# Column fetches, depth blocks and small sums put at other places in a one-core mLSTM and attention trunk

## The chip, the cores and the metric

The kernel runs on one core of a Trainium2 chip. The metric is the device time of one execution in microseconds (us). TensorE is called PE below, VectorE DVE, ScalarE ACT, SyncE SP.

## What is computed

Two layers act on x, 512 tokens of 2048 columns, in float32. Each layer normalises x over its columns, scales and shifts it by columns that are made from a conditioning vector c, runs a mixer, normalises the mixer's output and adds it to x, times a gate column. The first mixer is an mLSTM with 8 heads, the second an attention over bands of chunks with 16 heads, whose keys and values come from the stream after the first layer.

```
sc = silu(c)
for l in (0, 1):
    shift, scale, gate = split(sc @ ada_w[l] + ada_b[l])
    h = rmsnorm(x, g_pre[l]) * (1 + scale) + shift
    if l == 0:
        y = mlstm(h @ a_w_in) @ a_w_out                # 8 heads
    else:
        kshift, kscale = split(sc @ kv_ada_w + kv_ada_b)
        kv = (rmsnorm(x, kv_g) * (1 + kscale) + kshift) @ kv_w
        y = (band_attention(h @ b_w_in, kv) * silu(z)) @ b_w_out   # 16 heads
    x = x + gate * rmsnorm(y, g_post[l])
```

## The kernel before

**Precision and weights.** All projections are made from pairs of tiles: a number is split into a high part (an ACT cast, line 182) and a low part (a DVE subtraction, line 183), and a product is three matmuls: high by high, high by low, low by high (`mm3`, line 226). Weights lie in DRAM in the order of their use (`stream`, line 60). Each call of `wpiece` (line 188) takes the next piece: an SP transfer into a raw buffer (line 200; two buffers, and in some stages a third), then the split. All transfers are issued by SP, one after the other.

**Order.** The instructions are given to a scheduler that orders each engine's list by the program and by priorities (`tc.high_priority`). An instruction that is pinned (`pin`, `tc.keep_in_program_order`) stays behind what the program has put on its engine so far. What is not pinned may go ahead.

**Modulation columns.** The 128 groups of 128 columns (shift, scale and gate of the layers, shift and scale of the keys) are not made by PE. For each group a transfer brings rows of the transposed weights (`ada_load`, line 376, halves of 512 KB), and DVE multiplies them with a broadcast of silu(c) and sums (`ada_sum`, line 381, one instruction for a half). They are spread over the program as background work.

**Start** (lines 401 to 453). c is fetched, then the four quarters of x (line 409), 1 MB each, then constants and the first four halves of columns, for depth tile 0. PE broadcasts c and ACT makes silu(c) from it (line 420). ACT squares x, DVE adds the squares (lines 433 and 436), PE sums them over the partitions (`token_sums`, line 424), and the reciprocal root is spread over a tile by four small products and matmuls (`dg`, lines 448 to 450).

**First projection** (lines 460 to 477). Depth tiles k = 0 to 15 come in BLOCKS: 0-1, 2-5, 6-9, 10-13, 14-15. For each k, four column halves are loaded and summed and the input h is made (`modulated`, line 357: a DVE pass, an ACT pass, a DVE pass at line 360); then PE does the lead, 6 column tiles of weights (18 matmuls of 512 columns) that accumulate in six PSUM banks through all blocks. After the lead of a block, ten later column tiles follow with all k of the block; each is added by DVE to an accumulator in SBUF (line 477).

**Heads, then the first output projection.** Heads 0 to 7 run with columns as background. From each head's output, the square sum over its columns is split and summed by PE (`sums`, line 546; called at line 745). The output projection (`rows`, line 861) goes by groups g of 512 columns; a weight piece covers two depth tiles (24 matmuls with four row tiles). `proj_b` (line 245) calls a function at given depth steps k0 (its `at`). In g = 0 and in the first pair of row tiles of g = 1 to 3, `scale_sums` (line 872) is such a function: it sums the four quarters of scale columns that its last call loaded, and loads the next four. The inputs y of the projection are fetched piece by piece (line 777).

**Keys and values.** Values first, then eight key tiles with `proj_s` (line 266), which computes pairs of depth tiles with seven half products instead of eight (`seven`) where the sums of inputs are ready, and plainly (`eight`) elsewhere. KEY_PAIRS says for how many of eight pairs. `input_sums` (line 929) makes the sums of one more pair.

**Tail.** After attention comes `b_w_out`, again by groups g of 512 columns; group 3 goes in two halves, rows 0-1 and rows 2-3. `gate_steps` (line 1178) places the gate columns' loads and sums (`gate_sums`), their transposes (`gate_part`, which runs `gates_out`, line 572: a DVE product, a PE transpose, a store), the reading back as a row (`gate_row`), and the product with group 0's output (`gate_first`, line 1173). `fetch_x` (line 1126) fetches the stored stream; `finish` (line 1146) ends a row tile.

Of the kernel before, what the change touches and what calls it, by code (L numbers as in the profile page):

```python
# [15 lines left out]
P = 128  # L16
D = 2048
S = 512
# [17 lines left out]
PAIRS = [(0, 1), (2, 3)]  # L36
BLOCKS = [(0, 2), (2, 6), (6, 10), (10, 14), (14, 16)]
LEAD = [0, P, V0 // 2, V0 // 2 + P, O0, O0 + P]
# [3 lines left out]

KEY_PAIRS = [6, 7, 8, 8, 8, 8, 8, 8]
HEAD_PAIRS = 6
# [88 lines left out]
def hybrid_trunk(ctx, tc, xT, xN, c, adaT, cols, wst, wg, ext, kc, out):  # L133
# [42 lines left out]
    def col(i):  # L176
        return cl[:, i : i + 1]
# [176 lines left out]
    def newa(name):  # L354
        return psA.tile([P, S], F32, tag="a", name=name)
# [59 lines left out]
    early = [ada_load(KT, j, ap_, ADA_BUFS, pin) for j in range(2)]  # L415
    early += [ada_load(0, j, sp, 4, pin) for j in range(2)]
    for i in range(4):
        ps = newp(f"ps_c{i}")
        mm(ps, ones_f[0:1, :], crow[i], True, True)
        nc.scalar.activation(scB[:, i * S : (i + 1) * S], ps, AF.Silu)  # L420
    nc.sync.dma_start(csc, scB[0:1, :])
    pss = newa("ps_x")

# [4 lines left out]
    for q in range(4):  # L428
        pair = []
        for i in range(2):  # L430
            sq = xp.tile([P, 2, S], F32, tag="x", name=f"xsq{q}_{i}")
            nc.scalar.activation(sq, xq[q][:, 2 * i : 2 * i + 2, :], AF.Square)
            pin(nc.vector.tensor_tensor(sq[:, 0, :], sq[:, 0, :], sq[:, 1, :], op=ALU.add))
            pair.append(sq[:, 0, :])
        if q < 3:
            pin(nc.vector.tensor_tensor(pair[0], pair[0], pair[1], op=ALU.add))
            token_sums(pair[0], q == 0, False)
        else:
            token_sums(pair[0], False, False)
            token_sums(pair[1], False, True)  # L440
    rc = sp.tile([P, 4], F32, name="rc")
    nc.scalar.activation(rc, pss[:, 0:4], AF.Sqrt, bias=eps_c, scale=1.0 / D)
    for a in early[:2]:
        ada_sum(*a, pin)
    pin(nc.vector.reciprocal(rc, rc))
    psr = newa("ps_rb")
    for m in range(4):
        dg = tp.tile([P, S], F32, tag="t", name=f"dg{m}")[:, :P]
        pin(nc.vector.tensor_scalar(dg, ident, rc[:, m : m + 1], None, op0=ALU.mult))
        mm(psr[:, m * P : (m + 1) * P], ones_f, dg, m == 0, m == 3)  # L450
    nc.scalar.copy(rstd0, psr)
    for a in early[2:]:
        ada_sum(*a, pin)
    h1 = []
# [90 lines left out]

    def sums(ps, x, name, early=0):
# [4 lines left out]
        mm(ps, ones_r, t[:, 0, :], True, False)  # L551
        mm(ps, ones_r, t[:, 1, :], False, True)

# [77 lines left out]
    for h in range(NH):  # L631
# [239 lines left out]

    def scale_sums():

        for i, j, a in scale_in:
            pin(nc.vector.tensor_tensor_reduce(
                a, a, scQ[j], 1.0, mod[:, i : i + 1] if j else col(CB + i), ALU.mult, ALU.add, mod[:, i : i + 1]
            ))
        scale_in.clear()
        for i, j in scale_cols[:4]:
            d = slice(j * S, (j + 1) * S)  # L880
            if len(scQ) == j:
                scQ.append(tp.tile([P, S], F32, tag="t", name=f"scQ{j}"))
                pin(nc.sync.dma_start(scQ[j], csc[0, d].partition_broadcast(P)))
            a = tp.tile([P, S], F32, tag="t", name=f"adq{i}_{j}")
            pin(nc.sync.dma_start(a, adaT[i, :, d]))
            scale_in.append((i, j, a))
        del scale_cols[:4]
# [285 lines left out]
    def gate_first():  # L1173
# [83 lines left out]
```

## Time and profile before

| | |
|---|---|
| median of 3 runs (lowest, highest) | 2802.58 us (2798.52, 2809.12) |
| profiled execution, its own time | 2803.29 us |
| its span | 2801.5 us |
| PE, DVE, ACT busy | 99%, 77%, 49% of the span |
| moved by DMA | 527.09 MB, mean 188 GB/s |

A span is the time from the first to the last record of one execution. A busy share is an average over stages with different limits; a stage is read by windows of time. In a list of waits each row names the engine and line that stood still, what released it, the time in total, the number of times and the longest. In a timeline a row gives the start, the busy time, the engine, the line, the operation with output and inputs, how many were merged, and in brackets the idle time before it with what ended it. Matmuls overlap, so their merged busy times are longer than their pace.

### The profile page before, as it was taken

What the parts mean: (1) busy time and instruction counts of PE and PEld (TensorE: products, weight loads), DVE (VectorE), ACT (ScalarE), POOL (GpSimd) and SP (SyncE); (2) the same over time, 40 slices, a digit from 0 to 9 for tenths busy, and PEclk for the clock granted to TensorE, in tenths of its full rate; (3) what the DMA queues carried; (4) which work ended last, traced back from release to release, by engine and by line L of the source; (5) the groups of instructions that cost most, each with busy time, mean ns of one, the idle gap of its engine ahead of it and who ended that gap; (6) DMA issues with size and microseconds to landing.
All of it is one profiled execution on the core that took longest, in us unless ns stands there. A gap on an engine that the chain in (4) does not pass through costs nothing.

```text
span 2801.5 us, 42223 instructions
## 1 busy us (share of the span) xinstructions
PE 2765.5 (99%) x15959; PEld 2439.5 (87%) x15959; DVE 2156.6 (77%) x3788; ACT 1370.5 (49%) x2032; POOL 0.2 (0%) x4
## 2 busy tenths in 40 slices
PE   7999999999999999999999999999999999999998
PEld 5887888888998989989998788888998899999886
DVE  6986978769786876858867577567986788898666
ACT  4234524234454554545545344568534566666523
POOL 0000000000000000000000000000000000000000
PEclk9999999999999999999999999999999999999999
DMA  7875697865232332323324889778535534434876
GB/s 289 308 259 180 213 319 249 300 224 181 91 114 93 102 115 91 113 91 106 120 85 140 280 292 306 260 257 297 175 131 175 174 125 129 130 122 126 291 266 207
DMA packets 182999, 527.09 MB, mean 188 GB/s; under 512 B 19669, under 2 KB 38133, under 8 KB 182153
## 3 DMA queue, kind: packets, MB, share of 16 engines
q1 hardware_dynamic: 182794, 524.38, 55.4%
q8 instruction: 125, 2.05, 0.3%
q14 instruction: 80, 0.66, 0.1%
HBM read 490.69 MB, written 38.85 MB: 189 GB/s over the span
## 4 chain that ended last, share of the span: by engine, by line
PE 85%; DVE 6%; DMA 5%; issue 2%; ACT 2%; SPq 0%; DVEq 0%; ACTq 0%
PE ps_y L224 14%; PE ps_v L224 12%; PE ps_kv L224 5%; PE ps_azo L224 5%; PE ps_o L224 4%; PE ps_bzo L224 3%; PE ps_az L224 3%; PE ps_cz L224 3%; PE ps_dz L224 3%; PE ps_qk L224 3%; PE ps_z L224 3%; PE ps_czo L224 3%; PE ps_dzo L224 3%; PE ps_s L224 2%; DMA wr<-in_wst 2%
## 5 line engine op out<-in xcount | busy, mean ns | idle before, releaser
L182 ACT CAST wh<-wr 128x1024 fp32r<-128x1024 f32 (+3 forms) x586 | 585.4, 1001 | 709.5 <-PE ps_y L224 152.5
L183 DVE TENSOR_TENSOR wl<-wr,wh 128x1024 fp32r<-128x1024 f32 (+3 forms) x586 | 679.0, 1161 | 307.3 <-ACT wh L182 300.4
L224 PE MATMUL ps_y<-wh,y 128*128 128x512 f32 x1536 | 477.3, 390 | 1.3 <-ACT y L182 1.1
L182 ACT CAST wsh<-ws 128x384 fp32r<-128x384 f32 (+1 forms) x261 | 163.4, 626 | 372.7 <-issue 137.1
L224 PEld LDWEIGHTS ps_y<-wh,y 128*128 128x128 f32 x1536 | 288.2, 188 | 62.3 <-ACT y L182 1.5
L224 PE MATMUL ps_v<-wh,h 128*128 128x512 f32 x1024 | 322.1, 390 | 0.4 <-DVE zq L318 0.4
L224 PE MATMUL ps_y<-wl,y 128*128 128x512 f32 x768 | 299.2, 390 | 0.7 <-DVE wl L183 0.7
L183 DVE TENSOR_TENSOR wsl<-ws,wsh 128x384 fp32r<-128x384 f32 (+1 forms) x261 | 181.8, 696 | 125.8 <-ACT wsh L182 124.1
L224 PEld LDWEIGHTS ps_v<-wh,h 128*128 128x128 f32 x1024 | 192.3, 188 | 40.2 <-DVE zq L318 0.8
L224 PE MATMUL ps_v<-wl,h 128*128 128x512 f32 x512 | 199.6, 390 | 0.0
L224 PEld LDWEIGHTS ps_y<-wl,y 128*128 128x128 f32 x768 | 144.2, 188 | 30.6 <-DVE wl L183 1.2
L224 PE MATMUL ps_kv<-wh,hkv 128*128 128x512 f32 x512 | 159.4, 390 | 0.0
L207 DVE TENSOR_TENSOR ws<-wr 128x256 f32<-128x256 f32 (+1 forms) x261 | 132.1, 515 | 30.8 <-DMA wr<-in_wst 28.7
L382 DVE CUSTOM_DVE_ANT_0 ada<-ada,scB,mod 128x1024 f32<-128x1024 f32 x96 | 123.0, 1282 | 17.5 <-DMA ada<-in_adaT 16.6
L382 DVE CUSTOM_DVE_ANT_0 ada<-ada,scB,cl 128x1024 f32<-128x1024 f32 x96 | 122.9, 1281 | 14.7 <-DMA ada<-in_adaT 14.7
L224 PEld LDWEIGHTS ps_kv<-wh,hkv 128*128 128x128 f32 x512 | 96.1, 188 | 19.8
L224 PEld LDWEIGHTS ps_v<-wl,h 128*128 128x128 f32 x512 | 96.2, 188 | 19.7 <-issue 0.9
L224 PE MATMUL ps_azo<-h,wh 128*128 128x256 f32 (+1 forms) x406 | 101.4, 331 | 0.4 <-DVE zo L318 0.4
L224 PE MATMUL ps_l<-h,wh 128*128 128x512 f32 x320 | 99.2, 392 | 1.0 <-ACT oz L475 1.0
L224 PE MATMUL ps_kv<-wl,hkv 128*128 128x512 f32 x256 | 99.7, 390 | 0.0
L224 PE MATMUL ps_czo<-h1s,wsh 128*128 128x256 f32 x468 | 89.3, 283 | 0.0
L209 DVE TENSOR_TENSOR ws<-wr 128x128 f32<-128x128 f32 (+1 forms) x261 | 85.2, 336 | 3.6
(389 smaller groups left out, 6259.9 us busy)
## 6 DMA issues: line engine op xcount, KB each, us to landing
wr<-in_wst SPq DMA_DIRECT2D x520, 512.0 KB, 3.7
ada<-in_adaT SPq DMA_DIRECT2D x224, 512.0 KB, 5.9
adq<-in_adaT SPq DMA_DIRECT2D x64, 256.0 KB, 5.4
xt<-nsc SPq DMA_DIRECT2D x48, 256.0 KB, 3.7
yr<-ysc SPq DMA_DIRECT2D x16, 512.0 KB, 3.8
wr<-in_wst SPq DMA_DIRECT2D x30, 256.0 KB, 4.6
wr<-in_wst SPq DMA_DIRECT2D x16, 384.0 KB, 7.8
bsc<-in_ext SPq DMA_DIRECT2D x16, 320.0 KB, 6.4
```

The source lines that it names most:

```text
L182: nc.scalar.copy(hi, src)
L183: nc.vector.tensor_tensor(lo, src, hi.bitcast(F32), op=ALU.subtract)
L207: nc.vector.tensor_tensor(t[:, : 2 * w], r[:, w : 3 * w], r[:, : 2 * w], op=ALU.subtract)
L209: nc.vector.tensor_tensor(t[:, 2 * w :], r[:, 3 * w :], r[:, w : 2 * w], op=ALU.subtract)
L224: nc.tensor.matmul(ps, a, b, start=start, stop=stop)
L382: pin(nc.vector.tensor_tensor_reduce(at, at, (sc or scB)[:, j * D // 2 : (j + 1) * D // 2], 1.0, mod[:, i : i + 1] if j else col(CB + i), ...
```

## The change

- The constants `cols` and the first four column halves are fetched before x, and summed before anything of x. The last quarter of x comes in two halves; of its squares ACT makes two and DVE two. The four `dg` products write one tile.
- BLOCKS are 0-1, 2-4, 5-8, 9-12, 13-15.
- `scale_sums` loads two quarters a step at twice as many steps, and sums a batch two steps after its load; the last ones are summed at the beginning of the second pair of row tiles.
- The two matmuls of the last head's square sum get a lower priority.
- The first key tile no longer makes another input sum: KEY_PAIRS is 6, 6, 7, 8 and so on in place of 6, 7, 8, 8.
- Gate loads begin four depth steps earlier in group 0, and the later steps are put earlier; `gate_first` goes from the last half of group 3 to the half before it; the fetches of the stored stream are pinned and put at other steps.

```diff
-BLOCKS = [(0, 2), (2, 6), (6, 10), (10, 14), (14, 16)]
+BLOCKS = [(0, 2), (2, 5), (5, 9), (9, 13), (13, 16)]
...
-KEY_PAIRS = [6, 7, 8, 8, 8, 8, 8, 8]
+KEY_PAIRS = [6, 6, 7, 8, 8, 8, 8, 8]
...
+    pin(nc.sync.dma_start(cl, cols))
+    early = [ada_load(i, j, *where, pin) for j in range(2) for i, where in ((KT, (ap_, ADA_BUFS)), (0, (sp, 4)))]
...
-        pin(nc.sync.dma_start(t, xT[q]))
+        for d in [slice(0, 4)] if q < 3 else [slice(0, 2), slice(2, 4)]:
+            pin(nc.sync.dma_start(t[:, d, :], xT[q, :, d, :]))
...
-        if q == 1:
-            pin(nc.sync.dma_start(cl, cols))
     pin(nc.sync.dma_start(kcs, kc[:, :144]))
-    early = [ada_load(KT, j, ap_, ADA_BUFS, pin) for j in range(2)]
-    early += [ada_load(0, j, sp, 4, pin) for j in range(2)]
...
     nc.sync.dma_start(csc, scB[0:1, :])
+    for a in early:
+        ada_sum(*a, pin)
...
+            for i in range(2):
+                nc.scalar.activation(sq[i][:, 0, :], xq[q][:, 2 * i, :], AF.Square)
+                pin(nc.vector.tensor_tensor(sq[i][:, 1, :], xq[q][:, 2 * i + 1, :], xq[q][:, 2 * i + 1, :], op=ALU.mult))
...
-    for a in early[:2]:
-        ada_sum(*a, pin)
     pin(nc.vector.reciprocal(rc, rc))
     psr = newa("ps_rb")
+    dg = xp.tile([P, 4, P], F32, tag="x", name="dg")
...
-    for a in early[2:]:
-        ada_sum(*a, pin)
...
+        with tc.high_priority(-late):
+            mm(ps, ones_r, t[:, 0, :], True, False)
+            mm(ps, ones_r, t[:, 1, :], False, True)
...
-        sums(ps, sqs, f"q{h}", AHEAD if h == NH - 1 else 0)
+        sums(ps, sqs, f"q{h}", *((AHEAD, 80) if h == NH - 1 else ()))
...
+    def scale_sums(n=1):
+
+        while len(scale_in) > n:
+            for i, j, a in scale_in.pop(0):
...
-        for i, j in scale_cols[:4]:
+        batch = []
+        for i, j in scale_cols[:2]:
...
-    rows(0, range(4), y_tile, {k: scale_sums for k in (6, 12, 18, 24, 30)})
+    rows(0, range(4), y_tile, {k: scale_sums for k in (*range(4, 32, 4), 30)})
...
-            at = {k: scale_sums for k in ((6, 14, 22, 30) if g < 3 else (6, 14, 22))} if pair == 0 else {}
+            at = {k: scale_sums for k in range(2, 32, 4)} if pair == 0 else {}
             if pair == 0 and g == 3:
-                at[30] = lambda: (scale_sums(), amul_cols(2, 48 + KT, GPRE + KT))
+                at |= {28: scale_sums}
+            if pair == 1 and g == 1:
+                scale_sums(0)
+                amul_cols(2, 48 + KT, GPRE + KT)
...
-        at = {2: input_sums} if ready < KT // 2 else {}
+        at = {2: input_sums} if i and ready < KT // 2 else {}
...
-            nc.sync.dma_start(t[i], xsc[m, :, 2 * i * S : 2 * (i + 1) * S].rearrange("p (a t) -> p a t", a=2))
+            pin(nc.sync.dma_start(t[i], xsc[m, :, 2 * i * S : 2 * (i + 1) * S].rearrange("p (a t) -> p a t", a=2)))
...
-        0: {14: gate_begin},
-        1: {2: gate_sums, 6: gate_sums, 8: lambda: gate_part(1), 12: lambda: (gate_row(1, 1), gate_sums())},
-        2: {2: gate_sums, 4: lambda: gate_part(2), 6: gate_sums, 8: lambda: gate_row(1, 2), 12: gate_sums, 14: lambda: gate_part(3)},
-        3: {0: gate_sums, 4: lambda: gate_row(1, 3), 8: gate_sums, 10: lambda: gate_part(0), 14: lambda: gate_row(1, 0, late[1])},
+        0: {10: gate_begin},
+        1: {0: gate_sums, 4: gate_sums, 6: lambda: gate_part(1), 10: lambda: (gate_row(1, 1), gate_sums()), 12: lambda: fetch_x(0), 14: gate_sums},
+        2: {0: lambda: gate_part(2), 2: gate_sums, 4: lambda: (gate_row(1, 2), fetch_x(1)), 6: gate_sums, 8: lambda: gate_part(3), 10: gate_sums, 12: lambda: fetch_x(2), 14: gate_sums},
+        3: {0: lambda: gate_part(0), 2: lambda: (gate_row(1, 3), fetch_x(3)), 6: lambda: gate_row(1, 0, late[1]), 12: gate_first},
...
-            at = {2: gate_first, 4: lambda: finish(0), 6: lambda: finish(1)} if pair == PAIRS[1] else {}
-            if 0 < g < 3:
-                at = {k: lambda k=k: fetch_x(2 * (g - 1) + k // 12) for k in (2, 12)}
+            at = {4: lambda: finish(0), 6: lambda: finish(1)} if pair == PAIRS[1] else {}
```

More of the change, by code (lines that the diff above doesn't have):

```diff
@@ L428, in hybrid_trunk @@
     for q in range(4):
-        pair = []
+        sq = [xp.tile([P, 2, S], F32, tag="x", name=f"xsq{q}_{i}") for i in range(2)]
+        if q < 3:
+            for i in range(2):
+                nc.scalar.activation(sq[i], xq[q][:, 2 * i : 2 * i + 2, :], AF.Square)
+        else:
+            for i in range(2):
+                nc.scalar.activation(sq[i][:, 0, :], xq[q][:, 2 * i, :], AF.Square)
+                pin(nc.vector.tensor_tensor(sq[i][:, 1, :], xq[q][:, 2 * i + 1, :], xq[q][:, 2 * i + 1, :], op=ALU.mult))
         for i in range(2):
[L431 to L434, printed above, removed]
+            pin(nc.vector.tensor_tensor(sq[i][:, 0, :], sq[i][:, 0, :], sq[i][:, 1, :], op=ALU.add))
+            if q == 3:
+                token_sums(sq[i][:, 0, :], False, i == 1)
         if q < 3:
[L436 to L440, printed above, removed]
+            pin(nc.vector.tensor_tensor(sq[0][:, 0, :], sq[0][:, 0, :], sq[1][:, 0, :], op=ALU.add))
+            token_sums(sq[0][:, 0, :], q == 0, False)
     rc = sp.tile([P, 4], F32, name="rc")
     nc.scalar.activation(rc, pss[:, 0:4], AF.Sqrt, bias=eps_c, scale=1.0 / D)
-    for a in early[:2]:
-        ada_sum(*a, pin)
     pin(nc.vector.reciprocal(rc, rc))
     psr = newa("ps_rb")
+    dg = xp.tile([P, 4, P], F32, tag="x", name="dg")
     for m in range(4):
-        dg = tp.tile([P, S], F32, tag="t", name=f"dg{m}")[:, :P]
-        pin(nc.vector.tensor_scalar(dg, ident, rc[:, m : m + 1], None, op0=ALU.mult))
-        mm(psr[:, m * P : (m + 1) * P], ones_f, dg, m == 0, m == 3)
+        pin(nc.vector.tensor_scalar(dg[:, m, :], ident, rc[:, m : m + 1], None, op0=ALU.mult))
+        mm(psr[:, m * P : (m + 1) * P], ones_f, dg[:, m, :], m == 0, m == 3)
     nc.scalar.copy(rstd0, psr)
-    for a in early[2:]:
-        ada_sum(*a, pin)
     h1 = []
@@ L544, in conv, with sums @@
         return t
-    def sums(ps, x, name, early=0):
+    def sums(ps, x, name, early=0, late=0):
         t = hp.tile([P, 2, S], F32R, tag="qk", name=f"sp_{name}", bufs=4)
@@ L870, in hybrid_trunk @@
     scale_in, scQ = [], []
[L872 to L878, printed above, removed]
-        for i, j in scale_cols[:4]:
+    def scale_sums(n=1):
+        while len(scale_in) > n:
+            for i, j, a in scale_in.pop(0):
+                pin(nc.vector.tensor_tensor_reduce(
+                    a, a, scQ[j], 1.0, mod[:, i : i + 1] if j else col(CB + i), ALU.mult, ALU.add, mod[:, i : i + 1]
+                ))
+        batch = []
+        for i, j in scale_cols[:2]:
             d = slice(j * S, (j + 1) * S)
@@ L885, in scale_sums @@
             pin(nc.sync.dma_start(a, adaT[i, :, d]))
-            scale_in.append((i, j, a))
-        del scale_cols[:4]
+            batch.append((i, j, a))
+        del scale_cols[:2]
+        if batch:
+            scale_in.append(batch)
     gate_row(0, 0)
-    rows(0, range(4), y_tile, {k: scale_sums for k in (6, 12, 18, 24, 30)})
+    rows(0, range(4), y_tile, {k: scale_sums for k in (*range(4, 32, 4), 30)})
     for pair, ms in enumerate(PAIRS):
         for g in range(1, 4):
-            at = {k: scale_sums for k in ((6, 14, 22, 30) if g < 3 else (6, 14, 22))} if pair == 0 else {}
+            at = {k: scale_sums for k in range(2, 32, 4)} if pair == 0 else {}
             if pair == 0 and g == 3:
-                at[30] = lambda: (scale_sums(), amul_cols(2, 48 + KT, GPRE + KT))
+                at |= {28: scale_sums}
+            if pair == 1 and g == 1:
+                scale_sums(0)
+                amul_cols(2, 48 + KT, GPRE + KT)
             if pair == 1 and g == 1:
```

2 lines of the change are left out of this document (removed).

## The prediction

> **What bounds the kernel now.** I read the page first, then the waits of PE alone, then windows over the stages in which PE waited, then the timeline at each wait.
>
> ```profile
> span 2801.5 us, 42223 instructions
> PE 2765.5 (99%) x15959; PEld 2439.5 (87%) x15959; DVE 2156.6 (77%) x3788; ACT 1370.5 (49%) x2032; POOL 0.2 (0%) x4
> ```
>
> TensorE is busy for 99% of the span. The change removes almost no matmul, so it can win only the time in which PE stands still: 2801.5 - 2765.5 = 36 us, plus matmuls that run slowly. The profiled run took 2803.29 us (1.8 us outside its span); the median of the three runs is 2802.58 us. My sum goes against 2803.3.
>
> ```profile
> PE ps_lead L224 <- ACT h L359: 4.3, 3, 2.7
> PE ps_lead L224 <- ACT wh L182: 4.1, 1, 4.1
> PE ps_x L224 <- DVE xsq L436: 4.1, 1, 4.1
> ...
> PE ps_gg L579 <- DVE ggate L577: 1.7, 1, 1.7
> PE ps_q L224 <- ACT sp_q L182: 1.1, 1, 1.1
> PE ps_y L224 <- ACT y L182: 1.1, 1, 1.1
> PE ps_ck L224 <- DVE zk L315: 1.1, 1, 1.1
> ...
> PE ps_y L224 <- DVE wl L183: 0.7, 1, 0.7
> PE ps_ak L224 <- DVE zk L318: 0.7, 1, 0.7
> ```
>
> The columns are total, times, longest. No wait repeats for the whole kernel: there is a start (xsq, wh, h) and a handful of single waits of about 1 us. The start deserves windows.
>
> ```profile
> 0.00:10.00 10.00, 7.16 (x8) 2.48 (x8) 0.18 (x3) 3.64 (x6) 0.20 (x4) 1.00 0.69 264
> 10.00:20.00 10.00, 6.30 (x29) 6.22 (x29) 8.60 (x14) 8.88 (x10) 0.00 (x0) 1.00 1.01 397
> ...
> 57.00:82.00 25.00, 20.13 (x77) 14.70 (x76) 23.35 (x36) 6.78 (x11) 0.00 (x0) 0.93 0.83 301
> 82.00:108.00 26.00, 26.00 (x116) 21.56 (x115) 24.40 (x43) 7.92 (x12) 0.00 (x0) 1.00 0.95 330
> 108.00:165.00 57.00, 56.86 (x250) 46.49 (x249) 55.80 (x93) 15.82 (x24) 0.00 (x0) 1.00 0.93 318
> ```
>
> After the window come PE, PEld, DVE, ACT, POOL, then clock, DMA share, GB/s. From 108 to 165 PE does 250 matmuls in 56.86 us, 0.2275 us each; from 57 to 82 it does 77 where 110 would fit. VectorE is nearly full in both. So the first projection is limited by PE and VectorE almost equally: VectorE makes the inputs h of each depth tile k.
>
> **The change part by part.**
>
> *Start.* Four column transfers of 512 KB, 2.1 MB, and the constants move ahead of x; the same 6.5 MB (with 4.2 MB of x and 0.2 MB of constants) must have landed before the last x.
>
> ```profile
> 9.43 0.60 ACT L420 ACTIVATE scB<-ps_c 128x512 f32<-128x512 f32 x1 [1.11 <-PE ps_c L224]
> ...
> 13.52 9.11 PE L224 MATMUL ps_x<-ones_f,xsq 128*128 128x1 f32 x40 [4.12 <-DVE xsq L436]
> ...
> 17.15 1.28 DVE L433 TENSOR_TENSOR xsq<-xsq 128x512 f32<-128x512 f32 x2
> ...
> 18.35 1.28 DVE L382 CUSTOM_DVE_ANT_0 ada<-ada,scB,cl 128x1024 f32<-128x1024 f32 x1
> ...
> 26.32 0.75 DVE L358 SCALAR_TENSOR_TENSOR h1t<-xt,amul,ps_rb 128x512 f32<-128x512 f32 x1 [0.41 <-ACT ssum L451]
> ...
> 28.30 0.72 ACT L359 ACTIVATE h<-h1t,mod 128x512 fp32r<-128x512 f32 x1 [2.02 <-DVE mod L382]
> ...
> 29.80 1.22 PE L224 MATMUL ps_lead<-h,wh 128*128 128x512 f32 x2 [4.14 <-ACT wh L182]
> ```
>
> By the windows 2.64 MB land in the first 10 us and 3.97 MB in the next, so the last x comes at about 19.7 us. Behind it stand a product and a sum on VectorE (two such passes take 1.28 us), then two token sums on PE. Forty of their matmuls take 9.11 us, so a group of eight takes 1.8. That ends at 19.7 + 1.3 + 3.6 = 24.6, against 22.6 now: +2.0. In return the shift column is there early: h1t ended at 27.07 and h started at 28.30, because VectorE was summing that column; -1.2. Net +0.8; bounds -1.2 (x is not later after all) and +2.0 (another wait takes the place of the shift). The work moved, four sums of 1.28 us, waits for the broadcast of silu(c) (10.03 us) and holds VectorE until 15.2; the sums of the first quarters of x queue behind it and catch up before 19.7. The merged dg tile spares VectorE a buffer wait that PE's row sums cover: nothing.
>
> The Trainium skill, "DMA: Bandwidth & Descriptors", section Specifications, gives about 358 GB/s as the limit of HBM for one core. By that the last x would come at 20.8 us and the forecast would be 1.1 us more. The trace carries 397 GB/s over 10 us, so I keep the row.
>
> *Blocks 2, 3, 4, 4, 3.* Matmuls, weights and additions are the same in number. What moves is when each h is due.
>
> ```profile
> 57.26 0.74 PE L224 MATMUL ps_lead<-h,wh 128*128 128x512 f32 x2
> ...
> 70.07 2.50 PE L224 MATMUL ps_lead<-h,wh 128*128 128x512 f32 x5 [2.70 <-ACT h L359]
> ...
> 77.73 1.90 PE L224 MATMUL ps_lead<-h,wh 128*128 128x512 f32 x7 [1.38 <-ACT h L359]
> ...
> 156.40 0.75 DVE L360 SCALAR_TENSOR_TENSOR h<-h1t,mod,h 128x512 fp32r<-128x512 f32 x1
> ...
> 219.22 2.95 PE L224 MATMUL ps_g<-h,gw 128*32 128x512 f32 x12
> ```
>
> Now: the first block has 96 matmuls (21.8 us) and runs from 29.8 to 57.26, 5.6 lost. The second block's lead has 72 (16.4 us) and ends near 82, 8.5 lost: VectorE needs four sums of 1.28 us and two passes of 0.75 for each k, 6.6 us before any weight, PE only 18 x 0.2275 = 4.1. With three k in that block, k=5 gets 90 further matmuls (20 us) of cover. But every later due time moves forward too. The lead of k=12 would be due after 486 matmuls, at 29.8 + 5.6 + 110.6 = 146.0. VectorE finished that h (the thirteenth of line 360, 156.40) with its ACT half at about 155.6. At an unchanged pace PE waits there instead, less 18 matmuls (4.1 us) of two later columns that can go ahead. Then 282 matmuls (64.2 us) remain: 155.6 - 4.1 + 64.2 + 0.9 (small stalls as now) = 216.6, against 219.2: -2.6. Without those 18 it is +1.5. If VectorE runs ahead by the four sums it no longer does between 18 and 28 us (5.2 us), -7.8; PE's own limit is -8.2. VectorE idles some 5 us between 30 and 57 for late columns, so part of the head start is lost; I take the middle, **-5**, ends +1.5 and -8.2.
>
> *Scale columns.* The same 64 sums; two per step instead of four, summed two steps after their load.
>
> ```profile
> 1580.23 1.00 SPq L885 DMA_DIRECT2D adq<-in_adaT  x2
> ...
> 1582.72 0.33 SPq L777 DMA_DIRECT2D yr<-ysc  x1
> ...
> 1585.81 0.50 PE L224 MATMUL ps_y<-wh,y 128*128 128x512 f32 x1 [1.08 <-ACT y L182]
> ```
>
> SP issues in order: the y tile stood behind a batch of four and PE waited 1.08 us for it. A batch of two holds the queue half as long. I take -1; ends -1.4 and +35 (a rival below). Six buffers hold two batches, and a second scQ where the quarter changes.
>
> *Last head's square sum.* Its two matmuls are put behind projection work; the queue no longer stops for sp_q: **-1.1**. What is late next is head 7's y tiles, needed 14 weight pieces (24 matmuls, 5.5 us each) later; cost nothing, at worst the 1.1 back.
>
> *Key sums.* One fused pair fewer in the first two key tiles each in turn.
>
> ```profile
> 1440.00:1460.00 20.00, 20.00 (x147) 19.02 (x146) 15.96 (x35) 10.43 (x16) 0.00 (x0) 1.00 0.31 106
> 1980.00:2000.00 20.00, 18.26 (x140) 17.35 (x139) 19.90 (x37) 11.69 (x16) 0.00 (x0) 1.00 0.47 161
> ```
>
> VectorE is full (19.90 of 20) exactly where ps_ck and ps_ak wait, 1.8 us. Taking one input sum out of the first key tile clears that. Two pairs now take 12 full matmuls (2.73 us) instead of 21 halves (between half a full one, 0.114, and 20.00/147 = 0.136 in a stage that mixes both, so 2.4 to 2.9): -0.3 to +0.7, I take +0.5, as the mixture contains full ones. Sum **-1.3**, ends -2.1 and +0.7.
>
> *Tail.* Gate columns start two pieces earlier, so the transposes come earlier; the row products leave the last pass.
>
> ```profile
> 2764.08 1.28 DVE L382 CUSTOM_DVE_ANT_0 ada<-ada,scC,mod 128x1024 f32<-128x1024 f32 x1 [2.18 <-DMA ada<-in_adaT]
> ...
> 2766.64 0.27 PE L579 MATMUL ps_gg<-kcs,ggate 128*4 128x128 f32 x1 [1.73 <-DVE ggate L577]
> ...
> 2773.46 1.90 DVE L1176 TENSOR_TENSOR yo<-yo,gb 128x512 f32<-128x512 f32 x3 [1.30 <-DMA gb<-ggd]
> ...
> 2787.17 0.50 PE L224 MATMUL ps_y<-wl,y 128*128 128x512 f32 x1 [0.73 <-DVE wl L183]
> ```
>
> PE's queue stood 1.73 us behind a transpose whose column came late, and 0.73 us for a low part that VectorE did after the row products. Both go: **-2.4**. Pinning the fetches of x puts them behind weights in SP's queue, where they last had to be done by the last pass; a step with four columns, 1 MB of x and two weight pieces is 4.2 MB, 10.6 us at 397 GB/s, against 10.9 us of matmuls, so the cover is thin: ends -2.4 and +3.
>
> Sum: 0.8 - 5 - 1 - 1.1 - 1.3 - 2.4 = -10.0, so **2793.3 us**.
>
> **The rivals.**
> (B) VectorE uses its freed time for the columns of k=1, the waits at k=3, 4 and 5 go, and the start is not later: -1.2 - 8.2 - 5.8 = -15.2, 2788.1. For it: VectorE is idle while rstd is made. Against: k=2's columns queue behind weight transfers.
> (C) The change doesn't do what it says: columns land early but are not used early. Start +2, the wait moves to k=12 (+1.5), single waits go by half (-2.9): 2804.
> (D) Slower: scale loads hold SP's queue. There are 32 steps where there were 16. If each makes y or weights late as at 1585 (1.08 us), that is 34.6 in place of the -1: 2793.3 + 35.6 = 2829; if each second one does, 2812. It decides when a load waits for its buffer longer than the weights held ready last, two pieces or 10.9 us. Against: the oldest batch is summed just before.
>
> **How the numbers follow.** Half a per cent is 14 us, about what a measurement of this kernel can tell from no change: below 2788.6 is faster, above 2816.6 slower. Forecast 0.42 (own range 2788 to 2799), B 0.30 (2782 to 2790), C 0.17 (2798 to 2807), D 0.11 (2812 to 2830). Faster: 0.25 of B and 0.05 from the lower edge of the forecast, 0.30. Slower: what of D lies above the mark, 0.09. Same: the rest, 0.61. The range leaves out D and B's lower edge, under 0.2 in all: 2783 to 2809.
>
> **What would show it.** The first lead matmul near 30.6 instead of 29.80; no wait at k=5, but one at k=12 near 150 us; ps_g near 214 instead of 219.22; no rows ps_q, ps_ck, ps_gg in PE's waits. Wrong would be: new waits of ps_y for y, wh or wl between 1515 and 1800 us or after 2640; a start beyond 32 us; or a busy sum of PE that changed by more than 1 us.

## The result and the profile after

| | before | after |
|---|---|---|
| median (lowest, highest), 20 runs each, taken in turn | 2804.07 us (2798.52, 2810.16) | 2808.71 us (2804.93, 2814.15) |
| ratio, 95% interval | | 1.0018 [1.0011, 1.0025] |
| span of the profiled execution | 2801.5 us | 2812.1 us |

The change makes the kernel about 5 us **slower** (3 to 7 by the interval). The prediction said 10 us faster. The sign of the forecast is wrong. The time lies inside the stated range (2783 to 2809 us) by 0.3 us, a little above the band of rival C (2798 to 2807), so that it lies inside at all is luck. Both kernels lie within half a per cent of each other; with 20 runs a side the difference is resolved all the same. The profiled execution of after took 2813.87 us, 5 us more than the median of its kernel, and that of before 0.8 us less than its own, so the traces differ by more than the medians do.

The page of after, its span and its busy sums:

```profile
span 2812.1 us, 42209 instructions
PE 2767.8 (98%) x15941; PEld 2440.9 (87%) x15941; DVE 2157.3 (77%) x3790; ACT 1369.5 (49%) x2032; POOL 0.2 (0%) x4
```

PE is busy 2.3 us longer than before (2765.5), and stands still 44.3 us instead of 36.0. The waits of PE in after (engine, what it waited for, total, times, longest):

```profile
PE ps_x L224 <- ACT xsq L433: 9.5, 2, 8.8
PE ps_lead L224 <- ACT h L359: 5.8, 4, 2.2
PE ps_l L224 <- ACT wh L182: 4.4, 2, 3.4
PE ps_x L843 <- DVE xn L835: 3.2, 2, 3.0
...
PE ps_ck L224 <- DVE zk L315: 1.1, 1, 1.1
PE ps_y L224 <- ACT y L182: 1.1, 1, 1.1
PE ps_ak L224 <- DVE zk L318: 1.0, 1, 1.0
...
PE ps_kv L224 <- DVE wl L183: 0.8, 1, 0.8
...
PE ps_gg L580 <- DVE ggate L578: 0.2, 1, 0.2
```

Two of the rows that were to go are gone or nearly so (ps_q is not there, ps_gg fell from 1.7 to 0.2); ps_ck stays as it was. The larger ones are new or have grown: 9.5 us for the squares of x (4.1 in before), 4.4 us for weights behind the start of the first projection, 3.0 us for xn. The start, from the timeline of after:

```profile
7.18 1.28 DVE L382 CUSTOM_DVE_ANT_0 ada<-ada,scB,cl 128x1024 f32<-128x1024 f32 x1 [6.18 <-DMA ada<-in_adaT]
...
14.53 2.00 ACT L433 ACTIVATE xsq<-xt 128x1024 f32<-128x1024 f32 x2 [4.57 <-DMA xt<-in_xT]
...
17.03 2.00 ACT L433 ACTIVATE xsq<-xt 128x1024 f32<-128x1024 f32 x2 [0.50 <-DMA xt<-in_xT]
...
19.54 2.00 ACT L433 ACTIVATE xsq<-xt 128x1024 f32<-128x1024 f32 x2 [0.50 <-DMA xt<-in_xT]
...
22.91 1.28 DVE L437 TENSOR_TENSOR xsq<-xt 128x512 f32<-128x512 f32 x2
...
23.14 5.29 PE L224 MATMUL ps_x<-ones_f,xsq 128*128 128x1 f32 x24 [0.67 <-DVE xsq L443]
24.11 1.28 DVE L439 TENSOR_TENSOR xsq<-xsq 128x512 f32<-128x512 f32 x2
...
33.60 1.65 PE L224 MATMUL ps_lead<-h,wh 128*128 128x512 f32 x3 [2.21 <-ACT h L359]
```

In before ACT squared x from 9.93 us without a gap. Here it waits for x 4.57 us, and 0.5 us each for the second and the third quarter, which is squared from 19.54. The quarters come 2.5 us apart, so the last one comes at about 22.0 us (an estimate from that spacing; its second half is squared from 22.2 on without a wait). PE has 24 token-sum matmuls, three groups, left at 23.14 us, and ends them at 28.43 (22.63 in before). The first lead comes at 33.60 instead of 29.80, **3.8 us late**. The reader can see the gain that was hoped for as well: of the 5.8 us at the token sums 3.8 are left at the lead. The shift column gives 1.2 of the difference (0.78 us pass from the start of h1t to that of h, where 1.98 did), and 0.7 come from the first weights, whose cast now stands ahead of h.

The same windows as in the prediction, and one between (columns as there), first of after, then of before:

```profile
0.00:10.00 10.00, 7.16 (x8) 2.49 (x8) 1.98 (x6) 3.67 (x5) 0.20 (x4) 1.00 0.67 196
10.00:20.00 10.00, 1.84 (x8) 1.78 (x8) 7.17 (x13) 4.47 (x5) 0.00 (x0) 1.00 1.02 422
...
57.00:82.00 25.00, 22.05 (x86) 16.91 (x85) 19.07 (x31) 7.17 (x12) 0.00 (x0) 0.93 0.81 274
82.00:108.00 26.00, 23.82 (x105) 19.23 (x103) 24.50 (x43) 6.34 (x10) 0.00 (x0) 1.00 0.94 320
100.00:120.00 20.00, 14.40 (x54) 10.87 (x53) 16.28 (x28) 4.68 (x7) 0.00 (x0) 0.91 0.88 299
```

```profile
100.00:120.00 20.00, 20.00 (x90) 16.58 (x89) 20.00 (x34) 5.86 (x8) 0.00 (x0) 1.00 0.94 316
```

From 57 to 82 us PE does 86 matmuls instead of 77 (93 in e2 below, where the start is that of before): the stall at k=4 and 5 is milder, as meant, though not gone. But from 100 to 120 it does 54 instead of 90, and 36 x 0.2275 = 8.2 us are lost there. The timeline of after shows where, and its windows of 2 us the clock (the column before the last two):

```profile
103.96 1.88 PE L224 MATMUL ps_lead<-h,wh 128*128 128x512 f32 x7 [2.18 <-ACT h L359]
...
111.76 0.73 PE L224 MATMUL ps_l<-h,wh 128*128 128x512 f32 x2 [3.43 <-ACT wh L182]
112.39 2.64 PE L224 MATMUL ps_lead<-h,wh 128*128 128x512 f32 x7
...
225.44 6.89 PE L224 MATMUL ps_g<-h,gw 128*32 128x512 f32 x29
```

```profile
112.00:114.00 2.00, 2.00 (x8) 1.34 (x8) 2.00 (x4) 0.33 (x1) 0.00 (x0) 0.82 0.91 338
114.00:116.00 2.00, 2.00 (x6) 1.62 (x5) 2.00 (x6) 0.00 (x0) 0.00 (x0) 0.50 0.99 369
116.00:118.00 2.00, 2.00 (x9) 1.56 (x9) 0.59 (x1) 0.00 (x0) 0.00 (x0) 0.83 0.74 260
```

These are the leads of k=6 and 7, in the block 5-8: two waits of 2.18 and 3.43 us, and behind them a stretch at half the clock. The first projection ends (ps_g, the first matmul of the gates) at 225.44 instead of 219.22, 6.2 us late: 3.8 from the start and 2.4 more. What brings the weights late is the SP queue, and ahead of it VectorE; the timelines of SP and ACT in after:

```profile
95.44 7.43 SPq L378 DMA_DIRECT2D ada<-in_adaT  x4
102.96 5.41 SPq L200 DMA_DIRECT2D wr<-in_wst  x3
```

```profile
102.45 0.83 ACT L182 CAST wh<-wr 128x768 fp32r<-128x768 f32 x1 [4.95 <-DMA wr<-in_wst]
103.19 0.72 ACT L359 ACTIVATE h<-h1t,mod 128x512 fp32r<-128x512 f32 x1
...
110.36 1.35 ACT L182 CAST wh<-wr 128x768 fp32r<-128x768 f32 x2 [6.45 <-DMA wr<-in_wst]
111.61 0.72 ACT L359 ACTIVATE h<-h1t,mod 128x512 fp32r<-128x512 f32 x1
```

Four column loads hold SP's queue for 7.43 us, and the weights stand behind them. What SP's queue waited for at the column loads between 30 and 165 us, first in after, then in before, and below it the same between 90 and 116 us, again after and then before:

```profile
SPq L378 <- DVE mod L382: 18.3, 11, 4.3
SPq L378 <- DVE mod L382: 16.9, 8, 4.5
...
SPq L378 <- DVE mod L382: 10.3, 4, 4.3
SPq L378 <- DVE mod L382: 3.6, 1, 3.6
```

Line 378 is the column load, line 382 the column sum: a load needs a column buffer that VectorE has to sum first. Over the whole projection SP waits hardly longer than before; what differs is that most of it now falls ahead of the third block's leads.

The late weights hold up h as well, because the pass that makes h stands behind their cast in ACT's list. For k=6 its input h1t was ready at 100.10 us and h starts at 103.19; for k=7 it was ready at 109.96 and h starts at 111.61. But at k=7 PE had run out of work at 108.33 already, so there VectorE is late by itself too.

### The profile page after: what moved, and what is told of

Same layout as the page of the kernel before. It is cut to its first block, busy times and chain, and to the rows that moved or that the text cites. A ratio compares the mean times of both kernels' runs of the same rounds, so it can differ in the third digit from the quotient of the medians.

```text
span 2812.1 us, 42209 instructions
## 1 busy us (share of the span) xinstructions
PE 2767.8 (98%) x15941; PEld 2440.9 (87%) x15941; DVE 2157.3 (77%) x3790; ACT 1369.5 (49%) x2032; POOL 0.2 (0%) x4
## 4 chain that ended last, share of the span: by engine, by line
PE 85%; DMA 6%; DVE 4%; ACT 2%; issue 2%; SPq 0%; DVEq 0%; ACTq 0%
PE ps_y L224 13%; PE ps_v L224 12%; PE ps_azo L224 5%; PE ps_o L224 4%; PE ps_kv L224 4%; PE ps_bzo L224 3%; PE ps_l L224 3%; PE ps_az L224 3%; PE ps_cz L224 3%; PE ps_dz L224 3%; PE ps_qk L224 3%; PE ps_z L224 3%; PE ps_czo L224 3%; PE ps_dzo L224 3%; DMA wr<-in_wst 2%; PE ps_lead L224 2%
## 5 line engine op out<-in xcount | busy, mean ns | idle before, releaser
L182 ACT CAST wh<-wr 128x1024 fp32r<-128x1024 f32 (+4 forms) x586 | 585.3, 1000 | 700.5 <-PE ps_y L224 178.7
L183 DVE TENSOR_TENSOR wl<-wr,wh 128x1024 fp32r<-128x1024 f32 (+4 forms) x586 | 678.7, 1160 | 290.1 <-ACT wh L182 286.5
L224 PEld LDWEIGHTS ps_kv<-wh,hkv 128*128 128x128 f32 x512 | 96.2, 188 | 19.7
```

Of the source, the lines that this page charges most:

```text
L182: nc.scalar.copy(hi, src)
L183: nc.vector.tensor_tensor(lo, src, hi.bitcast(F32), op=ALU.subtract)
L224: nc.tensor.matmul(ps, a, b, start=start, stop=stop)
```

## The experiments

Ratios are against runs of the kernel before on the same chip, with 95% intervals. e1 to e5 put one part of the change alone into before (e5 two small ones); e6 to e8 and e12 take the start and the blocks apart; e9 to e11 look for a better kernel; e13 to e15 undo parts in after. Times within a run (lead, ps_g) are from one profiled execution each.

**e1, the start alone.** All hunks of the start (constants and four column halves ahead of x and summed first, last quarter in halves, one dg tile), nothing else.

```diff
+    pin(nc.sync.dma_start(cl, cols))
+    early = [ada_load(i, j, *where, pin) for j in range(2) for i, where in ((KT, (ap_, ADA_BUFS)), (0, (sp, 4)))]
...
+    for a in early:
+        ada_sum(*a, pin)
```

> The kernel before with the start of the change alone (columns ahead of x, split last quarter, one dg tile). Theory 1, x lands late behind 2.1 MB and PE then has three token sums of 1.8 us in a row: the first lead matmul near 33.5 us instead of 29.8, and the slip stays to the end, +2 to +5 us. Theory 2, VectorE uses the freed 5 us for k=1: the first lead is late by 3 to 4 us, but the waits at k=3 to 5 shrink by as much, and the gates (ps_g) begin within 1 us of 219.2; total within 1 us.

Measured: 2806.8 us, ratio 1.0009 [1.0000, 1.0018]. The lead moved as in after, in the timeline of e1:

```profile
33.88 0.80 PE L224 MATMUL ps_lead<-h,wh 128*128 128x512 f32 x1 [2.21 <-ACT h L359]
```

That is 4.1 us late; ps_g is 2.9 us late, the last ps_y 3.4. Most of the slip stays to the end. The start costs about 2.5 us by the ratio, whose interval begins at 1. The column sums that now stand ahead on VectorE are not what costs: in after the last of them ends at 13.66 us, before the first quarter of x is there.

**e2, the blocks alone.**

```diff
-BLOCKS = [(0, 2), (2, 6), (6, 10), (10, 14), (14, 16)]
+BLOCKS = [(0, 2), (2, 5), (5, 9), (9, 13), (13, 16)]
```

> The kernel before with the blocks 2, 3, 4, 4, 3 alone. Theory 1 of the prediction, the waits at k=4 and 5 shrink and one at k=12 appears: ps_g 2 to 5 us earlier than 219.2. Theory 2, weights queue on SP behind column loads that wait for their buffers, now in the block of k=5 to 8: 5 us of waits between 95 and 115 us, ps_g 0 to 3 us later.

Measured: 2807.74 us, 1.0011 [1.0003, 1.0020]. ps_g came 2.3 us later than in before. The waits of PE in e2 and a window of it:

```profile
PE ps_l L224 <- ACT wh L182: 4.3, 2, 3.8
PE ps_lead L224 <- ACT h L359: 3.1, 3, 1.3
```

```profile
100.00:120.00 20.00, 16.25 (x63) 12.42 (x62) 17.70 (x32) 3.23 (x5) 0.00 (x0) 0.91 0.83 283
```

The same hole as in after, with the start untouched; e13 has it too (a wait of 3.40 us at 106.48). The stall that leaves the second block comes back in the third, at k=6 and 7, and not at k=12.

**e3, the scale columns alone** (two quarters a step, summed two steps later).

```diff
-        for i, j in scale_cols[:4]:
+        for i, j in scale_cols[:2]:
...
```

> The kernel before with the scale columns in batches of two alone. Theory 1, the last batch is summed in the second pair's first tile, the residual's rows come late and the transposes of xn wait about 3 us: values (ps_kv) begin 2 to 4 us later than 1873.3, total +2 to +3. Theory 2, the waits of that stage in the profile of the change were chance: ps_kv within 1 us of 1873.3, total -1 to +1.

Measured: 2803.72 us, 1.0001 [0.9992, 1.0009]. The wait for y went, and PE waited 2.5 us for xn in its place: nothing is left of it in the total.

**e4, the tail alone** (gate steps, pinned fetches of x, gate_first earlier).

```diff
-        0: {14: gate_begin},
+        0: {10: gate_begin},
...
```

> The kernel before with the gate columns earlier, the fetches of x pinned and gate_first moved, alone. Theory 1, the two waits of the tail (1.7 and 0.7 us) go: the last matmul 2.4 us earlier than 2792.1, total -2 to -3. Theory 2, the gain seen between attention and the end in the profile of the change came from other parts: no change, within 1 us.

Measured: 2804.35 us, 0.9998 [0.9989, 1.0006]. From the last transpose of attention (ps_t) to the last ps_y the kernel took 167.2 us where before took 169.0, and the wait for ps_gg fell from 1.7 to 0.5 us. Kernels with the tail of before spread over nearly as much (below), and in the total nothing can be told.

**e5, the key parts alone** (one input sum fewer in the first key tiles, the last head's token sums at lower priority).

```diff
-KEY_PAIRS = [6, 7, 8, 8, 8, 8, 8, 8]
+KEY_PAIRS = [6, 6, 7, 8, 8, 8, 8, 8]
...
+        with tc.high_priority(-late):
```

> The kernel before with the two small order changes alone: KEY_PAIRS 6, 6, 7, 8 and the low priority of the last head's square sum. Theory 1 of the prediction: the waits of ps_q (1.1), ps_ck and ps_ak (1.8) go, 0.5 us of matmuls is added, total -2 to -3. Theory 2: VectorE is full in the first key tile from the splits and differences of weights, not from the one input sum; ps_ck and ps_ak stay at 1.5 to 2.5 us, and total is within 1.5 us of before.

Measured: 2803.6 us, 0.9995 [0.9986, 1.0004]. The wait for sp_q is gone. The waits at the end of the first key tile stay at 1.1 us (ps_ck) and 1.0 (ps_ak). So it is not the input sum that makes VectorE late there; what does was not taken apart.

**e6, the split of the last quarter alone**, with the columns behind x as in before.

```diff
-        pin(nc.sync.dma_start(t, xT[q]))
+        for d in [slice(0, 4)] if q < 3 else [slice(0, 2), slice(2, 4)]:
+            pin(nc.sync.dma_start(t[:, d, :], xT[q, :, d, :]))
...
```

> The kernel before with only the split of x's last quarter into halves and of its squares between ScalarE and VectorE; the columns stay behind x. If the column order alone makes the start late (theory 1), the first lead matmul is at 28.5 to 29.8 us, no later than before. If the split or its added VectorE work makes it late (theory 2), it is at 31 to 34 us.

Measured: 2803.63 us, 1.0000 [0.9991, 1.0009], first lead at 29.97 us. The split is not what costs; the order of the transfers is.

**e7, new blocks with half of VectorE's column work.** For k from 1 the sums go over half of their products, which leaves out half of the shift and scale columns; all transfers stay.

```diff
-                for a in ada_start(k):
-                    ada_sum(*a)
+                for i, j, a in ada_start(k):
+                    nc.vector.tensor_tensor_reduce(
+                        a[:, : D // 4], a[:, : D // 4], scB[:, j * D // 2 : j * D // 2 + D // 4], 1.0,
...
```

> New blocks alone, and in the first projection for k of 1 and more each column sum runs over half of its 1024 products (the rest is left out): all transfers stay, VectorE has 0.5 us less in each of 60 sums. If VectorE's time bounds that stage, the waits between 95 and 115 us (5 us) go and the gates begin 6 us or more before those of the blocks alone (221.5), near 212 to 215. If the transfers bound it, the waits stay and the gates begin within 3 us of 221.5.

Measured: 2799.11 us, 0.9987 [0.9978, 0.9996]; ps_g at 213.03 us, 8.5 earlier than in e2. The window of e7:

```profile
100.00:120.00 20.00, 19.66 (x86) 15.74 (x85) 15.56 (x32) 6.32 (x10) 0.00 (x0) 1.00 0.84 290
```

The hole is closed with the transfers as they were, and SP's queue waits much less at the column loads; the rows between 30 and 165 us of e7 (e2 has 19.4 us for VectorE's sums):

```profile
SPq L378 <- DMA ada<-in_adaT: 3.7, 1, 3.7
SPq L378 <- DVE mod L464: 0.8, 1, 0.8
```

VectorE's column work sets the first projection. A queue that is held does not make the hole by itself: here, too, four column loads hold SP for 7.62 us, from 86.38 on, and ACT then idles 4.87 and 4.46 us for weights, but PE waits only 0.34 us in the third block.

**e8, new blocks with half of the column bytes.** Each half column brings 256 KB instead of 512 and is summed twice (so half of the columns' weights stay unused); VectorE has two sums of 0.75 us for one of 1.28.

> New blocks alone, and in the first projection for k of 1 and more each column transfer brings half (256 KB, the rest is left out), summed twice, so that VectorE has at least as much work as before: two sums of 0.75 instead of one of 1.28. If transfers bound the stage, the waits between 95 and 115 us go and the gates begin 4 us or more before 221.5. If VectorE's time bounds it, the waits grow and the gates begin 5 to 15 us after 221.5.

Measured: 2806.81 us, 1.0009 [1.0000, 1.0018]; ps_g at 221.17 us. The window of e8, with a DMA share of 0.47 where e2 has 0.83:

```profile
100.00:120.00 20.00, 17.33 (x68) 13.24 (x68) 18.44 (x48) 3.07 (x5) 0.00 (x0) 0.91 0.47 159
```

The hole stays with half of the bytes, 3.9 us of waits where e2 has 5.0; mostly its name changes, from wh (0.5 us left) to h (3.4). So it is not bandwidth. Since this kernel gives VectorE 0.22 us more per sum, it alone would not settle that; with e7 it does. My rival had expected a much later end than came.

**e9, tail and key parts together** (e4 and e5 in one kernel).

> Before with the key parts (6, 6, 7 input sums, the last square sum's token sum taken later) and the gate columns' new places, start, blocks and scale columns as before. Theory 1 (waits that went are worth their length): the 1.1 us of ps_q and 1.1 to 1.8 us at the end add to a ratio near 0.9990, about -2.5 us. Theory 2 (an identical stage differs by up to 3 us from one execution to the next and waits of 1 us are not worth their length): ratio within 0.9995 to 1.0005.

Measured: 2801.18 us, 0.9992 [0.9984, 1.0001]. That is what e4 and e5 give when added (0.9993), but the interval takes in 1: a gain is not shown.

**e10, one group of token sums fewer.** An edit that neither kernel has: the last quarter, too, is summed to one tile on VectorE.

```diff
-        if q < 3:
-            pin(nc.vector.tensor_tensor(pair[0], pair[0], pair[1], op=ALU.add))
-            token_sums(pair[0], q == 0, False)
-        else:
-            token_sums(pair[0], False, False)
-            token_sums(pair[1], False, True)
+        pin(nc.vector.tensor_tensor(pair[0], pair[0], pair[1], op=ALU.add))
+        token_sums(pair[0], q == 0, q == 3)
```

> Before with one edit that neither kernel has: the last quarter of x is summed to one tile on VectorE (one sum of 0.6 us more), so that TensorE has 32 token-sum matmuls of 0.2275 us and not 40. Theory 1 (at the start of before TensorE's token sums, 9.11 us back to back, are the chain): they end 1.7 us earlier, near 20.9 us, the first ps_lead comes at 28.1 to 28.5 us instead of 29.80, ratio 0.9994 or so. Theory 2 (the shift column's sums or the transfers are the chain): first ps_lead within 0.4 us of 29.80.

Measured: 2802.32 us against 2805.35, **0.9989 [0.9981, 0.9998]**, about 3 us faster than before, though the interval ends close to 1. The timeline of e10:

```profile
13.46 7.63 PE L224 MATMUL ps_x<-ones_f,xsq 128*128 128x1 f32 x32 [4.12 <-DVE xsq L435]
...
28.41 1.22 PE L224 MATMUL ps_lead<-h,wh 128*128 128x512 f32 x2 [4.14 <-ACT wh L182]
```

The token sums end at 21.09 instead of 22.63, the first lead is 1.4 us earlier, and ps_g 4.4 us earlier (214.77); of the latter 1.7 us are a stretch of slow clock that before has at 70 us and this run lacks (below). e3, whose first projection is that of before, lacks the stretch as well and has ps_g at 216.44, 1.7 us behind e10. The chain at the start of before is the token sums on PE, as theory 1 said.

**e11, e9 and e10 in one.**

> The two kernels before in one: key parts, gate columns' places and the last quarter summed to one tile; start's transfers, blocks and scale columns as before. Theory 1 (gains add): first ps_lead 28.1 to 28.5 us, no row of ps_q, ps_gg at 0.6 us or less, ratio 0.9985 (about -4 us). Theory 2 (given back in later waits): ratio 0.9995 to 1.0005.

Measured: 2801.96 us, 0.9991 [0.9982, 1.0000]. The start is that of e10 (first lead 28.39), ps_q's wait is gone, but there are a wait of 2.2 us for y and one of 2.3 us for ps_gg, where 0.6 at most was expected. Whether more is gained than by e10 alone can't be told.

**e12, half of the bytes ahead of x**: constants and the scale column's two halves only.

```diff
+    pin(nc.sync.dma_start(cl, cols))
+    early = [ada_load(KT, j, ap_, ADA_BUFS, pin) for j in range(2)]
     xt, xq = [], []
```

> Before with the column constants and only the scale column's two transfers (1 MB) ahead of x, the shift column's two behind it; x in whole quarters. Theory 1 (x comes late by the bytes ahead of it): the first square on ScalarE starts at 11.9 to 12.6 us (9.93 in before, 14.81 with four transfers ahead), and the first ps_lead near 31.5 to 32.2 us (29.80 and 33.88). Theory 2 (the order alone costs, whatever the bytes, or the column sums standing ahead on VectorE do): first ps_lead within 0.5 us of 33.88 or of 29.80.

The timeline of e12:

```profile
11.56 2.00 ACT L431 ACTIVATE xsq<-xt 128x1024 f32<-128x1024 f32 x2 [1.60 <-DMA xt<-in_xT]
...
31.87 1.65 PE L224 MATMUL ps_lead<-h,wh 128*128 128x512 f32 x3 [3.41 <-ACT h L359]
```

First lead 2.1 us late with two transfers ahead, 4.1 with four: x is late by what stands ahead of it. It is not by the bytes alone: the first square starts at 11.56 us with two (11.9 to 12.6 was expected) and at 14.81 with four (e1), against 9.93, which is not in proportion. Of e12 there is one run, so its total is not compared.

**e13, e14, e15: after with the start, the blocks, and both as in before.** These undo the hunks of e1 and e2 in the changed kernel. They were to tell whether the two losses add or hide each other, and whether anything else is lost.

> After with the start of before (new blocks, key parts, scale columns and gate columns stay). If the costs of start and blocks add as they stood alone (ratios 1.0009 and 1.0011 against before) and the other parts give nothing: ratio against before 1.0005 to 1.0011, ps_g 2 to 3 us later than in before (6.2 in after). If either cost hides the other (the first projection waits for VectorE in any case): ratio 1.0015 to 1.0020, as after, and ps_g 5 to 6 us later.

> After with the depth blocks of before (its start, key parts, scale columns and gate columns stay). If the costs add: ratio 1.0004 to 1.0010, first ps_lead 4 us later and ps_g 2.5 to 4 us later than in before. If either hides the other: ratio 1.0015 to 1.0020, ps_g 5 to 6 us later.

> After with start and blocks of before: only scale columns, key parts and gate columns are new. If start and blocks are the whole loss: ratio 0.9988 to 1.0000, ps_g within 0.5 us of before. If what is left of the loss lies in the other parts together (none showed it alone): ratio above 1.0005, and the profile has a wait of over 2 us behind 1515 us that before lacks.

| | ratio against before | ps_g against before |
|---|---|---|
| after | 1.0018 [1.0011, 1.0025] | +6.2 us |
| e13, start of before | 1.0003 [0.9995, 1.0012] | +1.7 us |
| e14, blocks of before | 1.0013 [1.0004, 1.0022] | +2.2 us |
| e15, both of before | 1.0001 [0.9993, 1.0010] | -0.4 us |

With both undone nothing of the loss is left that these runs resolve. The trace of e15 does have a wait of 2.9 us for xn that before lacks, but its ratio shows nothing of it.

The first projection is the same program in before, e3, e4, e5, e9 and e15, and ps_g comes there between 216.44 and 219.54 us; with one of the two edits (e1 and e14, e2 and e13) it comes between 220.91 and 222.12, with both at 225.44. So each edit makes it late, and the two do not hide each other: hiding would have left it near 222. That the costs simply add fits, but is not shown in the total: e13 came out below its band of 1.0005 to 1.0011 and e14 between its two bands, and its interval takes in both. Start and blocks account for the loss, and the other three parts are worth nothing that these runs resolve.

## Why the prediction was wrong, step by step

- **Start (+0.8; measured +3.8).** The failed step is "the last x comes at about 19.7 us. Behind it stand a product and a sum on VectorE [...], then two token sums on PE". The bytes were counted rightly, but not when they land. In the first 10 us after moved 196 GB/s where before moved 264, and all four quarters slip: the third is squared only from 19.54, the last comes at about 22.0, 2.3 us later than was reckoned. VectorE, in order, comes to its product at 22.91, and PE has three groups left, 5.29 us, instead of two, which is the other 1.5: the token sums end at 28.43, not 24.6. The -1.2 for the early shift column came out as forecast; another 0.7 us were gained at the first weights. The forecast named a start "beyond 32 us" as what would prove it wrong; it was 33.60.
- **Blocks (-5; measured +2.3 alone).** The mechanism up to the second block was right: the stall at k=4 and 5 shrank. The failed step is "one at k=12 near 150 us", and under it "At an unchanged pace PE waits there instead". The prediction gave VectorE the pace that it had in before. But the block of three leaves 10 x 3 x 3 = 90 later-column matmuls (20.5 us) of cover where there were 120 (27.3 us), and the next debt falls due one block on, at k=6 and 7. There VectorE doesn't keep its pace either: from 100 to 120 us it is busy 16.28 us in after, where it was busy all 20.00 in before (1.43 us of its idle time lie ahead of the second wait, waiting for the h that late weights hold up, and 2.29 behind it). The end +1.5 of the step's own range was near, but by luck, for a wait at another place. e7 shows the root: with half of the column sums the hole is gone. Moving the due times of a short engine gave it no time.
- **What the prediction lacked: the queue.** In the third block PE does not wait for h alone but for plain weights, 3.43 us. VectorE's lateness keeps the column buffers occupied, SP stands at the column loads, the weights queue behind them, and without weights VectorE has nothing to split. The same coupling is in before; its length there fitted under the longer cover. That order of cause is read from the traces; e7 shows its first link, and more column buffers, which would cut the second, were not tried. e8 bounds the second link: with only 0.5 us of waits for weights left, 3.4 us of waits for h remain. The prediction looked for such a coupling only in the scale columns (rival D), where it did not occur.
- **Scale columns (-1).** In after the wait for y is there as before (1.1 us), and xn is waited for 3.0 us at 1777 us, where before waits 0.2. The trace of e3 shows the row loads of the residual 1.6 to 2.0 us late on VectorE there. e3's ratio is 1.0001: the gain was not there. Rival D did not come.
- **Last head's square sum (-1.1).** The wait went, in each kernel with this part. Its worth in the total is not resolved.
- **Key sums (-1.3).** The failed step is "Taking one input sum out of the first key tile clears that": ps_ck and ps_ak still wait 1.1 and 1.0 us. VectorE is full there without it (10.00 of 10 us from 1990 to 2000 in e9).
- **Tail (-2.4).** The waits went as forecast: none is left in after behind 2740 us, and from the last ps_t to the last ps_y after takes 166.4 us, 2.6 less than before. But before is at the long end. The ten traces with its tail lie between 167.4 and 169.1 us (mean 168.3), the seven with the new tail between 166.4 and 169.9 (mean 167.3; in e11 a wait of 2.3 us for ps_gg came back). So about 1 us is gained, not 2.4, and that the one pair of traces gives the forecast number is in part luck.
- **The mark for PE's busy sum** ("changed by more than 1 us") was too narrow: e3 and e4 run the same 15959 matmuls as before (2765.5 us) in 2763.2 and 2769.3 us.
- **The rivals.** The measured kernel is nearest to C ("columns land early but are not used early", the wait moves, single waits go by half), with a dearer start than its +2 and the wait at another place. B, VectorE ahead, is refuted by the late start and the hole, and e7 shows why: VectorE is the engine that is short.

The sum of the parts as they ran alone, 1.0009 + 1.0011 + 1.0001 + 0.9998 + 0.9995 less 4, is 1.0014, inside the interval of after.

## What to carry to other kernels

Ask of a load that is put first not only when the last byte behind it lands but when each piece lands, and count every pass that then stands bunched behind the late pieces, on each engine in its order. Where two engines are equally full, moving due times moves the wait to the next place with less cover; only work taken off the short engine (e7), or a shorter chain (e10), takes it away. And a queue that issues loads in order ties together what the program keeps apart: loads that wait for a slow consumer's buffers hold back the weights behind them, and with the weights whatever stands behind their cast (h, here by 3.1 and 1.7 us). Last, before a difference of 2 us between two traces is read as the work of a change, look at how far traces of the same program differ.

## What the runs showed of the hardware

**Behind some waits the clock dips, which costs 1.7 us more.** By windows of 2 us, the dips of the granted clock in the middle of these kernels have one size: the clock goes to 0.50, and what it lacks sums up to 1.70 or 1.72 us, which is 3.4 us at half speed (in e13 there are two in a row). In after there is one behind the wait at 111.76 us (rows above) and one at 72 us, in before one at 68 to 74 us. But the same wait need not bring one. The waits for ps_ck and ps_ak in the first key tile are 1.06 and 0.68 us in before, and 1.17 and 0.69 in e6, whose program is the same there; the windows of before and of e6, and a shorter one of e6:

```profile
1900.00:2000.00 100.00, 98.26 (x539) 84.98 (x539) 85.29 (x150) 77.92 (x122) 0.00 (x0) 1.00 0.78 261
```

```profile
1900.00:2000.00 100.00, 96.34 (x504) 82.05 (x504) 83.08 (x148) 76.32 (x121) 0.00 (x0) 0.98 0.79 260
```

```profile
1994.00:1996.00 2.00, 2.00 (x6) 1.59 (x6) 2.00 (x4) 0.83 (x1) 0.00 (x0) 0.50 0.55 221
```

The first row keeps 1.00, the second 0.98, and the third shows the dip in e6. e2, e4, e7, e8, e9 and e14 have the dip there too; before, after, e1, e3, e5, e10 to e13 and e15 do not. The Trainium skill, "TensorE: Matmul & The Clock Gate", section "Part 1: The HAM clock gate", says that the clock is halved after an idle window of about 3.4 us and that this window runs free of the kernel. The length of the dips (3.4 us at 0.50) agrees, and a free-running window would explain why the same waits bring a dip in one execution and not in another. If an idle window means one without any matmul, that does not agree: in e6 PE stood still 1.17 and 0.69 us with matmuls between.

**Stages with the same program differ by up to 4 us between executions.** The values' stage, from the first ps_kv to the first ps_dk, took 91.4 us in before, 91.2 in e3, 93.7 in e6, 93.8 in e4 and 95.3 in e9, at a clock of 1.00 in each, and none of these kernels changes it. What makes that difference stays open. Single waits of about 1 us lie below it, so a difference between two profiles in such a stage is no sign of the change.

**Transfers.** From 10 to 20 us after moved 422 GB/s, above the 397 of before on which the prediction rested. But in the first 10 us it moved 196 GB/s (194 in e1, with the same start) where before moved 264, so that 6.2 MB had come by 20 us instead of 6.6. The slow stretch is from 5 to 8 us: 188, 180 and 233 GB/s in the three windows of after, 401, 434 and 451 in those of before, 262, 393 and 381 in e12, with two column transfers ahead of x instead of four. Why the transfers run slower there was not found.
